# A transformer block on one core: the attention part recorded and then ordered by the builder for all five engines

## The chip, the core and the metric

The kernel runs on one core of one Trainium2 chip. The core has five instruction queues that run beside each other: TensorE (PE, matrix products and transpositions), VectorE (DVE), ScalarE (ACT), GpSimd (POOL) and SyncE (SP, which here only issues DMAs). Each engine runs its instructions in the order in which the program has them and waits at semaphores for results of the others. The metric is the device time of one execution in microseconds (us), the median of several runs.

## The reference

One block of an encoder: 512 tokens, 1024 features, float32, one layer. A normalisation and one input projection feed sixteen attention heads of three kinds; their outputs go through one output projection, then follow a gated MLP with a causal convolution and a gated per-layer embedding.

```python
hn = rms_norm(h, ln_mix[i])
z = hn @ w_in[i]
(q1, q2, k1, k2, va, qf, kf, vf, fg, qc, kc, vc) = jnp.split(z, IN_SPLITS, axis=-1)
...
o_a = diff_attention(q1, q2, k1, k2, va, lam, subln_gain[i], lam_init)
log_f = jax.nn.log_sigmoid(fg + fgate_bias[i])
o_b = forgetting_attention(qf, kf, vf, log_f)
o_c = chunk_attention(qc, kc, vc, rel_bias[i])
h = h + jnp.concatenate([o_a, o_b, o_c], axis=-1) @ w_out[i]
h = h + conv_gated_mlp(rms_norm(h, ln_ffn[i]), w_up[i], conv_w[i], conv_b[i], w_down[i])
gate = jax.nn.sigmoid(rms_norm(h, ln_ple[i]) @ w_ple_gate[i])
h = h + (p[i] @ w_ple_proj[i]) * gate
```

Every q and k is normalised per head. Group A (4 heads) takes the difference of two softmax maps, group B (6 heads) adds a cumulative sum of log forget gates to the scores, group C (6 heads) a bias by relative position.

## The kernel before

**Numbers.** Each float32 operand is split into a high and a low half of a faster type (`hi`, `lo`; `Th`, `Tl` for the tokens), and a product is three matmuls: hi hi, hi lo, lo hi (`mm3`). The high half of a weight is a cast on ScalarE; the low half is a subtraction on VectorE, on GpSimd, or a DMA that adds into the buffer (`load_w`, line 121 and on; the table entries "w..." say which).

**Stages.** First the input projection of the head pair A0, its weights in eight slices `WA`, while the tokens still arrive (`first_products`, line 289). The eight token blocks `xt` and the slices come by SP's queue (`load_k`, lines 245 to 250), slice 0 and the small columns by ACT's. All four token blocks' accumulators are open there, and slice k is used by twelve matmuls. Then nine more parts of the input projection (A0b, A1, A1b, B0 to B2, C0 to C2) in units of one part and one block of 128 tokens: eight steps of three matmuls each, then an evacuation with sums of squares (`qk_sums`, line 364: ACT squares, DVE sums, POOL scales and takes a power at line 373) and a scaling by DVE into `zn` (`qk_scale`). The steps of the heads are laid between the steps of these units: `qk_cols` turns q and k into columns by transpositions on PE (`split_q`, `split_k`, with moves on POOL at line 388), `scores` makes score products and softmax rows (the exponentials' tile is `e`; POOL scales it at lines 569 and 572), `prob_cols` transposes the rows (line 585), `values` multiplies them with V. `forget_cumsum` transposes the gates (`pf`), sums along the row on DVE (`fs`), sends the sums to DRAM and transposes them back (`pq`). The output projection `out_unit` runs in the same way in two column halves of four token blocks; its heads 12 to 15 come last (`last_out`). The MLP and the embedding behind it are recorded and ordered by a list scheduler of their own; the change doesn't touch them.

**What sets the order.** The table `T` gives for each step of a head its slot (a unit of a projection) and the place in it; `run` (line 691) deals them out. PE's order is the order in which the program is recorded, pinned instruction by instruction (`keep_in_program_order`). ACT and DVE are pinned only inside `first_products`; some DMAs are pinned too. For the rest the framework's scheduler chooses, with priorities: the table `EARLY` (line 726) and `step` raise those of some steps. Weights of the next part are loaded in pieces after each unit of this one. The buffers of the pools `ap` and `pi` and the accumulator banks are given out by the framework.

## Time and profile before

| what | value |
|---|---|
| median of 3 runs | 728.02 us (727.94 to 728.28) |
| profiled execution | 725.14 us |
| its span, first to last instruction | 723.4 us |
| granted clock of TensorE, mean | 0.999 |
| VectorE busy | 77% |
| ScalarE busy | 54% |
| GpSimd busy | 37% |
| DMA | 83.22 MB, mean 115 GB/s |

The profile is that of one execution. Its engine rows give the busy time of each engine; a row of the timeline gives the start, the length, the engine, the line and the tiles, and in brackets how long the engine was idle just before and what ended that. Nearly every instruction is recorded at one helper's line (78), so places are told by the tiles' names. From 4.4 to about 24 us runs the first projection, up to about 240 us the other projections with the heads, up to about 279 us the first part of the output projection with the last heads; behind it the rest of the output projection, the MLP and the embedding.

### The profile page before, as it was taken

What the parts mean: (1) busy time and instruction counts of PE and PEld (TensorE: products, weight loads), DVE (VectorE), ACT (ScalarE), POOL (GpSimd) and SP (SyncE); (2) the same over time, 40 slices, a digit from 0 to 9 for tenths busy, and PEclk for the clock granted to TensorE, in tenths of its full rate; (3) what the DMA queues carried; (4) which work ended last, traced back from release to release, by engine and by line L of the source; (5) the groups of instructions that cost most, each with busy time, mean ns of one, the idle gap of its engine ahead of it and who ended that gap; (6) DMA issues with size and microseconds to landing.
All of it is one profiled execution on the core that took longest, in us unless ns stands there. A gap on an engine that the chain in (4) does not pass through costs nothing. (4 is left out here: it accounts for less than half of the span.)

```text
span 723.4 us, 11848 instructions
## 1 busy us (share of the span) xinstructions
PE 703.0 (97%) x4204; PEld 631.1 (87%) x4204; DVE 555.8 (77%) x1090; ACT 393.9 (54%) x745; POOL 265.8 (37%) x355
## 2 busy tenths in 40 slices
PE   7998999999999999999999999999999999999997
PEld 7988889898999887889888899888998888899886
DVE  7788787987878845768969868787888779988552
ACT  6756676775666664565555444543444543544821
POOL 4675775756755540211102034021510004361400
PEclk9999999999999999999999999999999999999999
DMA  9544514414221145464445334552263322123541
GB/s 329 198 114 111 146 55 107 139 31 111 86 67 37 59 81 166 162 204 100 150 129 126 110 91 127 133 151 66 88 186 107 95 87 90 50 73 94 157 130 58
DMA packets 36950, 83.22 MB, mean 115 GB/s; under 512 B 4214, under 2 KB 6262, under 8 KB 36892
## 3 DMA queue, kind: packets, MB, share of 16 engines
q1 hardware_dynamic: 32844, 73.52, 32.3%
q0 software_dynamic: 3760, 8.66, 6.3%
q8 instruction: 33, 0.54, 0.3%
q10 hardware_dynamic: 288, 0.30, 0.1%
q14 instruction: 25, 0.20, 0.1%
HBM read 74.19 MB, written 4.21 MB: 108 GB/s over the span
## 5 line engine op out<-in xcount | busy, mean ns | idle before, releaser
L78 DVE TENSOR_TENSOR w_lo<-w_raw,w_hi 128x768 fp32r<-128x768 f32 (+1 forms) x118 | 113.9, 985 | 19.3 <-ACT w_hi L78 18.7
L78 ACT CAST w_hi<-w_raw 128x768 fp32r<-128x768 f32 (+1 forms) x118 | 89.6, 786 | 68.2 <-POOL w_raw L78 30.0
L78 PE MATMUL u<-Tl,w_hi 128*128 128x512 f32 (+1 forms) x336 | 125.5, 374 | 0.8 <-DVE Tl L78 0.8
L78 PE MATMUL u<-Th,w_hi 128*128 128x512 f32 (+1 forms) x336 | 125.7, 374 | 0.1
L78 PE MATMUL u<-Th,w_lo 128*128 128x512 f32 (+1 forms) x336 | 125.3, 373 | 0.0
L78 POOL TENSOR_TENSOR w_raw<-w_raw,w_raw 128x768 f32<-128x768 f32 (+1 forms) x30 | 53.9, 1818 | 148.4 <-DVE w_lo L78 116.1
L78 PEld LDWEIGHTS u<-Tl,w_hi 128*128 128x128 f32 x336 | 63.0, 188 | 13.0 <-DVE Tl L78 1.2
L78 PEld LDWEIGHTS u<-Th,w_lo 128*128 128x128 f32 x336 | 63.0, 188 | 12.6
L78 PEld LDWEIGHTS u<-Th,w_hi 128*128 128x128 f32 x336 | 63.0, 188 | 12.4 <-ACT pps L78 0.5
L78 DVE SCALAR_TENSOR_TENSOR c<-u,cols,c 128x511 f32<-128x511 f32 x76 | 56.7, 747 | 19.6 <-ACT c L78 18.4
L78 POOL DMA_DIRECT2D w_raw<-in_w_up_dram x9 | 7.9, 908 | 97.5 <-DMA w_raw<-in_w_up_dram 91.9
L78 ACT ACTIVATE c<-u,cols 128x512 f32<-128x512 f32 x38 | 29.5, 777 | 23.7 <-PE u L78 23.7
L78 PE MATMUL dn_X<-w_hi,g_ah 128*128 128x256 f32 x144 | 40.7, 283 | 0.3 <-DVE h L78 0.3
L78 PE MATMUL dn_X<-w_lo,g_ah 128*128 128x256 f32 x144 | 40.6, 282 | 0.3 <-DVE w_lo L78 0.3
L78 PE MATMUL dn_X<-w_hi,g_al 128*128 128x256 f32 x144 | 40.5, 281 | 0.0
L78 PE MATMUL B_z<-B_h,Th 128*128 128x384 f32 x96 | 34.5, 360 | 0.7 <-ACT B_l L78 0.7
L78 PE MATMUL C_z<-C_h,Th 128*128 128x384 f32 x96 | 34.3, 357 | 0.0
L78 PE MATMUL B_z<-B_h,Tl 128*128 128x384 f32 x96 | 32.3, 337 | 0.0
L78 PE MATMUL C_z<-C_h,Tl 128*128 128x384 f32 x96 | 32.3, 337 | 0.0
L78 PE MATMUL C_z<-C_l,Th 128*128 128x384 f32 x96 | 32.3, 336 | 0.0
L78 PE MATMUL B_z<-B_l,Th 128*128 128x384 f32 x96 | 32.3, 336 | 0.0
L78 PEld LDWEIGHTS dn_X<-w_hi,g_ah 128*128 128x128 f32 x144 | 27.1, 188 | 0.9 <-ACT w_hi L78 0.5
(482 smaller groups left out, 2139.1 us busy)
## 6 DMA issues: line engine op xcount, KB each, us to landing
w_raw<-in_w_up_dram SPq DMA_DIRECT2D x50, 384.0 KB, 3.8
w_raw<-in_w_down_dram SPq DMA_DIRECT2D x24, 384.0 KB, 3.1
w_raw<-in_w_up_dram SPq DMA_DIRECT2D x22, 256.0 KB, 3.5
B_r<-in_w_in_dram SPq DMA_DIRECT2D x12, 384.0 KB, 3.6
C_r<-in_w_in_dram SPq DMA_DIRECT2D x12, 384.0 KB, 3.2
wo_r<-in_w_out_dram SPq DMA_DIRECT2D x16, 256.0 KB, 2.9
w_raw<-in_w_ple_gate_dram SPq DMA_DIRECT2D x16, 256.0 KB, 3.0
h<-in_x_dram SPq DMA_DIRECT2D x4, 512.0 KB, 7.0
```

The costliest lines, as they stand in the source:

```text
L78: ins = getattr(self.eng, op)(*a, **k)
```

## The change

Every call on an engine between the first loads and the end of the attention part is now recorded in a plan instead of being issued (`Engine.__getattr__` and `Plan.add`). The plan keeps for each operation what it reads and writes by region, so what it depends on. `price` gives it a duration, on ACT and DVE 4% and on POOL 25% above its formula. `due` lays PE's operations end to end in recorded order and works back from there to the time by which each operation of another engine is due. `solve` then runs through time: the engine that is free first takes, of its ready operations, the one due first. PE takes only what has been ready for 0.15 us if there is such an operation, so it may pull later products ahead; ACT, DVE and POOL may hold back for a more urgent operation that is about to become ready. `emit` issues everything in that order and pins it, on all five engines. Three start values go with it: the times from which slice 0, the small columns and the identity are there, kept by the name of the tile.

The buffers come from `Fixed`: a fixed turn of tiles per tag, each held until its last reader. The table `EARLY`, the priorities and the waits for the first stage are gone. The loads of a part's weights are recorded after the units of the part before, not between them. The eight slices `WA` lie in other buffers: slices 0 and 1 in one `zn` tile, 2 and 3 in the other, the rest in tiles of the softmax rows. In `T` one entry moves, `A1v1` from (24, 7) to (24, 0).

Three places show how the order moves. The first is the head of SyncE's queue. `waq_92` is slice 1 before, `xbbias_86` the fifth block of tokens; after, `zn_91` holds slices 0 and 1, `zn_92` slices 2 and 3, and `bias_86` is the fifth block of tokens. Before:

```order
L249 DMA h<-in_xt_dram 128x257
L249 DMA h<-in_xt_dram 128x256
L249 DMA oall<-in_xt_dram 128x512
L250 DMA waq_92<-in_w_in_dram 128x384
L249 DMA oall<-in_xt_dram 128x512
L250 DMA waq_93<-in_w_in_dram 128x384
L249 DMA oall<-in_xt_dram 128x512
L250 DMA waq_94<-in_w_in_dram 128x384
L249 DMA xbbias_86<-in_xt_dram 128x512
```

and after:

```order
L261 DMA h<-in_xt_dram 128x257
L261 DMA h<-in_xt_dram 128x256
L261 DMA oall_71<-in_xt_dram 128x512 x2
L261 DMA zn_92<-in_w_in_dram 128x384
L261 DMA oall_71<-in_xt_dram 128x512
L261 DMA zn_92<-in_w_in_dram 128x384
L261 DMA bias_86<-in_xt_dram 128x512
L261 DMA zn_91<-in_w_in_dram 128x384
```

Slice 1 moves from the fourth load to the ninth. ScalarE casts it after the casts of slices 2 and 3 instead of ahead of them; PE's order of the first products is the same.

The second place is PE's queue at the forget sums (`pf`, `pq`; the banks of the changed kernel are named by their pool, `t_142` for the last of `pf`, `t_145<-ident,bias_87` for `pq`). Before:

```order
L78 MATMUL pf<-ident,oall 128x128 x4
L78 MATMUL A_z_787<-A_1_h,Th_64 128x384
L78 MATMUL A_z_787<-A_1_l,Th_64 128x384
L78 MATMUL A_z_787<-A_1_h,Tl_66 128x384
L78 MATMUL pq<-ident,fs 128x128 x4
```

and after:

```order
L261 MATMUL t_142<-ident,oall_71 128x128
L261 MATMUL z_125<-whi_102,Th_64 128x384
L261 MATMUL z_125<-wlo_103,Th_64 128x384
L261 MATMUL z_125<-whi_102,Tl_66 128x384
L261 MATMUL z_125<-whi_102,Th_64 128x384
L261 MATMUL z_125<-wlo_103,Th_64 128x384
L261 MATMUL z_125<-whi_102,Tl_66 128x384
L261 MATMUL z_125<-whi_104,Th_65 128x384
L261 MATMUL z_125<-wlo_105,Th_65 128x384
L261 MATMUL z_125<-whi_104,Tl_67 128x384
L261 MATMUL z_125<-whi_104,Th_65 128x384
L261 MATMUL t_145<-ident,bias_87 128x128 x4
```

Ten products of the projection stand between the two groups of transpositions where three stood. A little further on the probabilities of the first head are transposed. Before, block 3 of a bank follows block 2 at once:

```order
L78 MATMUL A_0_pt_865<-ident,A_0_0_e 128x128
L78 MATMUL A_0_pt_865<-ident,A_0_1_e 128x128
L78 MATMUL A_0_pt_865<-ident,A_0_2_e 128x128
L78 MATMUL A_0_pt_865<-ident,A_0_3_e 128x128
L78 MATMUL A1b_z_852<-A1b_h,Th_65 128x256
```

After, the blocks (`e_0_93`, `e_1_160`, `e_1_157`) alternate with products, score products follow, and block 3 (`e_0_95`) comes 20 rows after the first; the last rows of that stretch:

```order
L261 MATMUL z_124<-whi_112,Th_64 128x256
L261 MATMUL s_126<-kl_0_123,q_154 128x256
L261 MATMUL z_124<-wlo_113,Th_64 128x256
L261 MATMUL t_146<-ident,e_0_95 128x128
L261 MATMUL z_124<-whi_112,Tl_66 128x256
L261 MATMUL t_142<-ident,e_0_95 128x128
L261 MATMUL z_124<-whi_115,Th_65 128x256
```

The third place is PE's queue in the output projection, at the fifth of six steps of the first token block in the second column half (`wo_1_0` before, bank `z_124` after; `z_125` takes the next token block). Before:

```order
L78 MATMUL wo_1_0_3647<-wo_1_h,Th_64 128x512
L78 MATMUL wo_1_0_3647<-wo_1_l,Th_64 128x512
L78 MATMUL wo_1_0_3647<-wo_1_h,Tl_66 128x512
L78 MATMUL wo_1_0_3647<-wo_1_h,Th_65 128x512
L78 MATMUL wo_1_0_3647<-wo_1_l,Th_65 128x512
L78 MATMUL wo_1_0_3647<-wo_1_h,Tl_67 128x512
```

and after:

```order
L261 MATMUL z_124<-whi_104,Th_65 128x512
L261 MATMUL z_125<-whi_115,Th_64 128x512
L261 MATMUL z_125<-wlo_116,Th_64 128x512
L261 MATMUL z_125<-whi_115,Tl_66 128x512
L261 MATMUL z_125<-whi_118,Th_64 128x512
L261 MATMUL z_125<-wlo_119,Th_64 128x512
L261 MATMUL z_125<-whi_118,Tl_66 128x512
L261 MATMUL z_125<-whi_100,Th_64 128x512
L261 MATMUL z_125<-wlo_101,Th_64 128x512
L261 MATMUL z_124<-wlo_105,Th_65 128x512
L261 MATMUL z_124<-whi_104,Tl_67 128x512
```

Between the product with the high half `whi_104` and the one with its low half `wlo_105` now stand eight products of the next block.

```diff
--- before.py
+++ after.py
...
+class Plan:
+    WRITES = ("out", "accum_out")
+    LEAD = {"act": 0.035, "dve": 0.035, "pool": 0.095, "pe": 0.055, "sp": 0.1}
+    def __init__(self, clock, there):
+        self.group = "first"
+        self.clock, self.there, self.ops, self.mem = clock, {v.tensor.name: t for v, t in there}, [], {}
...
+    def add(self, eng, name, a, k):
+        op = Op(eng, name, a, k)
...
+        op.ready = 0.0
+        for w, v in sorted(seen, key=lambda x: x[0]):
+            r = self.region(v)
+            p0, p1, c0, c1 = r
+            log = self.mem.setdefault(v.tensor.name, [])
+            op.ready = max(op.ready, self.there.get(v.tensor.name, 0.0))
...
+        op.pos, op.group = len(self.ops), self.group
+        self.ops.append(op)
+        self.price(op)
+    def price(self, op):
+        e, k = op.eng.name, op.k
+        n = self.width(op.outs[0])
+        cols = sum(1 for v in op.ins if self.width(v) == 1) - (op.name == "reciprocal")
+        acc = "accum_out" in k
+        op.move = 0
+        if e == "pe":
+            if op.name == "transpose":
+                op.busy = 0.109
+            else:
+                op.busy = n * 0.0004556 + 0.001 if op.ins[0].dtype == F32R else n * 0.0017
+            op.lag = 0.165
+        elif e == "act":
+            op.busy, op.lag = 0.06 + n * 0.00088 + (0.18 + 0.04 * cols if acc else 0.09 * cols), 0.1
+        elif e == "dve":
+            n = max([n] + [self.width(v) for v in op.ins])
+            op.busy, op.lag = 0.07 + n * 0.001045 * (1 + (op.name == "tensor_tensor_scan")) + 0.06 * cols, 0.083
+        elif op.name == "dma_start":
+            op.move = n * 4 * op.outs[0].shape[0]
+            op.busy, op.lag = (0.9 if e == "pool" else 0.45), 0.0
+        elif op.name == "tensor_tensor":
+            op.busy, op.lag = ((0.42 + n * 0.155) if k["op"] == ALU.pow else (0.1 + n * 0.0024)), 0.04
...
+        else:
+            op.busy, op.lag = 0.08 + n * 0.00103 + (0.12 if n > 8 else 0.2) * cols, 0.04
+        op.busy *= self.SPARE.get(e, 1.0)
+    HW, SW, AT_ONCE = 0.385e6, 0.105e6, 8
+    SURE, AHEAD, MUCH, WAIT = 0.15, 1.0, 2.0, 0.6
+    SPARE = {"act": 1.04, "dve": 1.04, "pool": 1.25}
...
+    def due(self, shift):
+        t = 4.5
+        for op in self.ops:
+            if op.eng.name == "pe":
+                op.dl = t + shift.get(op.group, 0.0)
+                t += op.busy
+        for op in reversed(self.ops):
+            if op.eng.name != "pe":
+                spent = op.busy + op.lag + 0.05 + (op.move / self.HW + 2.0 if op.move else 0.0)
+                op.dl = min([q.dl for q in op.next], default=t) - spent
+    def solve(self):
+        clock = dict(self.clock)
+        free = {e: [] for e in self.ENGINES}
+        for op in self.ops:
+            op.left, op.at = len(op.deps), op.ready + self.LEAD[op.eng.name]
+            if not op.left:
+                free[op.eng.name].append(op)
+        wire, out, order = {"sp": 0.0, "pool": 0.0}, {"sp": [], "pool": []}, []
+        rank = lambda q: (q.dl, q.pos)
+        while True:
+            best = None
+            for e in self.ENGINES:
+                if free[e]:
+                    t = max(clock[e], min(q.at for q in free[e]))
+                    if best is None or t < best[0]:
+                        best = t, e
+            if best is None:
+                break
+            t, e = best
+            can = [q for q in free[e] if q.at <= t]
+            if e == "pe":
+                can = [q for q in can if q.at + self.SURE <= t] or can
+            op = min(can, key=rank)
+            if e not in ("pe", "sp"):
+                soon = [q for q in free[e] if t < q.at < t + op.busy * self.AHEAD and q.dl < op.dl - self.MUCH]
+                if soon:
+                    u = min(soon, key=rank)
+                    short = [q for q in can if t + q.busy <= u.at + 0.05]
+                    if short:
+                        op = min(short, key=rank)
+                    elif u.at - t < self.WAIT:
+                        op = u
+            free[e].remove(op)
+            t0 = max(clock[e], op.at)
+            busy = op.busy * (1.85 if e == "pe" and t0 < 8.6 else 1.0)
+            if op.move:
+                done = out[e]
+                if len(done) >= self.AT_ONCE:
+                    t0 = max(t0, done[-self.AT_ONCE])
+                wire[e] = max(t0 + 1.7, wire[e]) + op.move / (self.HW if e == "sp" else self.SW)
+                op.end = wire[e] + 0.6
+                done.append(op.end)
+            else:
+                op.end = t0 + busy + op.lag
+            op.start = t0
+            clock[e] = t0 + busy
+            order.append(op)
+            for q in op.next:
+                q.left -= 1
+                q.at = max(q.at, op.start if e == "pe" and q.eng is op.eng else op.end + self.LEAD[q.eng.name])
+                if not q.left:
+                    free[q.eng.name].append(q)
...
+        return order
+    def emit(self):
+        for op in self.ops:
+            for d in op.deps:
+                d.next.append(op)
+        for op in self.choose():
+            op.eng.now(op.name, op.a, op.k)
...
+    PLAN = []
     class Engine:
-        def __init__(self, eng):
-            self.eng, self.pinned, self.last = eng, False, None
+        def __init__(self, name, eng):
+            self.name, self.eng, self.pinned = name, eng, False
         def __getattr__(self, op):
             def do(*a, **k):
-                ins = getattr(self.eng, op)(*a, **k)
-                self.last = getattr(ins, "ins", None)
-                if self.pinned:
-                    tc.keep_in_program_order(ins)
-                return ins
+                if PLAN:
+                    return PLAN[-1].add(self, op, a, k)
+                return self.now(op, a, k, self.pinned)
             return do
...
+        def now(self, op, a, k, pinned=True):
+            ins = getattr(self.eng, op)(*a, **k)
+            if pinned:
+                tc.keep_in_program_order(ins)
+            return ins
+    pe, act, dve, pool, sp = (Engine(*e) for e in (("pe", nc.tensor), ("act", nc.scalar), ("dve", nc.vector), ("pool", nc.gpsimd), ("sp", nc.sync)))
+    class Fixed:
+        def __init__(self, pool, size={}, kind={}):
+            self.pool, self.size, self.kind, self.turn, self.made = pool, size, kind, {}, {}
+        def tile(self, shape, dt, tag, bufs=1, name=None):
+            i = self.turn[tag] = self.turn.get(tag, -1) + 1
+            key = tag, i % bufs
...
+            return v
...
+    banks = Fixed(ps)
     def bank(tag, name):
-        return ps.tile([P, 512], F32, tag=tag, bufs={"z": 2, "s": 2, "t": 3, "o": 1}[tag], name=name)
+        return banks.tile([P, 512], F32, tag, {"z": 2, "s": 2, "t": 3, "o": 1}[tag])
...
-    ap = p1.__enter__()
+    ap = Fixed(p1.__enter__())
...
-    WA = [ap.tile([P, S], F32, tag=tag, bufs=4, name=f"wa{tag}{i}")[:, :384] for tag in "qk" for i in range(4)]
-    def load_k(k, eng=nc.sync):
+    WA = [ap.tile([P, 1024], F32, tag="zn", bufs=2) for _ in range(2)]
+    WA = [t[:, i * 384 : (i + 1) * 384] for t in WA for i in range(2)]
+    WA += [ap.tile([P, n], F32, tag=tag, bufs=2)[:, :384] for tag, n in (("e2", 384), ("e2", 384), ("e3", 512), ("e3", 512))]
+    def load_k(k):
         parts = [(h[:, 3, c], xt0[:, c]) for c in (slice(0, H + 1), slice(H + 1, S + 1))] if k == 0 else [(XB[k], xt[k])]
         for dst, src in parts:
-            tc.keep_in_program_order(nc.sync.dma_start(out=dst, in_=src))
-        tc.keep_in_program_order(eng.dma_start(out=WA[k], in_=w_in[0][k // 2][:, k % 2, :]))
+            sp.dma_start(out=dst, in_=src)
+        if k:
+            sp.dma_start(out=WA[k], in_=w_in[0][k // 2][:, k % 2, :])
...
+    PLAN.append(Plan({"act": 2.95, "dve": 0.9, "pool": 1.0, "sp": 0.73, "pe": 1.0}, ((WA[0], 3.85), (cols, 4.6), (ident, 2.6))))
+    for k in range(KD):
         load_k(k)
...
-            qk_scale(z, ZN[pr, part], t, rs or evac())
+            rs = rs or evac()
+            if (pr, part) not in ZN:
+                ZN[pr, part] = ap.tile([P, NT, 2 * P], F32, tag="zn", bufs=2, name=f"{name}_zn")
+            qk_scale(z, ZN[pr, part], t, rs)
...
-        "A1v0": (22, 6), "A1s12": (21, 3), "A1p1": (23, 1), "A1v1": (24, 7), "A1n": (27, 7), "B0a": (22, 2),
+        "A1v0": (22, 6), "A1s12": (21, 3), "A1p1": (23, 1), "A1v1": (24, 0), "A1n": (27, 7), "B0a": (22, 2),
...
         for t in range(NT):
-            run(in_unit(pr, part, n, t, ws, pre[t]), steps.get(slot, []))
+            run(f"in{j}_{t}", in_unit(pr, part, n, t, ws), steps.get(slot, []))
             slot += 1
...
+        if j + 1 < len(PARTS):
+            q = PARTS[j + 1]
+            ws = [f() for f in in_w(j + 1, lo_by(q[0] + "ab"[q[1]], 4))]
+        else:
+            for k in range(6):
+                wo_load(k, 0)
...
+    PLAN.pop().emit()
```

More of the change, by code (lines that the diff above doesn't have):

```diff
@@ new lines, with again @@
+    class Fixed:
[4 more added lines that the diff above has]
+            key = tag, i % bufs
+            n = 1
+            for x in shape[1:]:
+                n *= x
+            if dt == BF16:
+                n //= 2
+            if key not in self.made:
+                kind = self.kind.get(tag, F32 if dt == BF16 else dt)
+                self.made[key] = kind, self.pool.tile([P, self.size.get(tag, n)], kind, tag=f"{tag}_{i % bufs}", name=f"{tag}_{i % bufs}")
+            kind, t = self.made[key]
+            v = t[: shape[0], :n]
+            if kind != dt:
+                v = v.bitcast(dt)
+            if len(shape) == 3:
+                v = v.rearrange("p (a b) -> p a b", a=shape[1])
+            return v
+        def again(self, tag, bufs, dt):
+            i = self.turn[tag] % bufs
+            return self.pool.tile([P, self.made[tag, i][1].shape[1]], dt, tag=f"{tag}_{i}", name=f"{tag}_{i}_again")
@@ L163, in in_turn @@
                 tag = ("hi", "lo")[(len(ring) - W["raw"]) % 2]
-            ring.append(pi.tile([P, 768], F32 if what == "raw" else F32R, tag=f"w{tag}", bufs=W[tag], name=f"w_{what}{len(ring)}"))
+            t = pi.tile([P, 768], F32 if tag == "raw" else F32R, tag=f"w{tag}", bufs=W[tag])
+            ring.append(t if tag == what else pi.again(f"w{tag}", W[tag], F32))
         else:
```

209 lines of the change are left out of this document (107 added, 102 removed), and 5 rows, old and new, of the table EARLY.

## The prediction

> **What bounds the kernel now.** I read the page's totals and slices first, then busy time by stretch, then what TensorE (PE) waits for.
>
> ```profile
> span 723.4 us, 11848 instructions
> PE 703.0 (97%) x4204; PEld 631.1 (87%) x4204; DVE 555.8 (77%) x1090; ACT 393.9 (54%) x745; POOL 265.8 (37%) x355
> PE   7998999999999999999999999999999999999997
> ```
>
> PE is busy 97% of the span, so a reordering that leaves every instruction in place can only win what PE waits, or lose by adding waits. The profiled execution took 725.14 us, 1.7 more than its span and 2.9 less than the median of 728.02; the sum below is made on 725.14 and the 2.9 are put back. The changed part ends on PE near 279 us; behind it the instruction sequence of PE is the same in both kernels.
>
> ```profile
> core 0: us, PE busy (x) PEld busy (x) DVE busy (x) ACT busy (x) POOL busy (x), PEclk, DMA share, GB/s
> 24.00:120.00 96.00, 90.95 (x591) 85.04 (x590) 80.09 (x227) 63.25 (x148) 63.75 (x90) 1.00 0.41 111
> 120.00:200.00 80.00, 78.20 (x482) 73.27 (x481) 66.55 (x219) 52.97 (x123) 55.67 (x83) 1.00 0.31 86
> 200.00:240.00 40.00, 39.88 (x247) 38.67 (x247) 32.20 (x95) 28.47 (x75) 22.55 (x40) 1.00 0.17 47
> 240.00:279.00 39.00, 37.65 (x196) 31.06 (x195) 22.53 (x54) 19.89 (x46) 15.72 (x22) 1.00 0.37 95
> 325.00:620.00 295.00, 294.67 (x1698) 257.03 (x1697) 242.94 (x334) 142.58 (x210) 58.83 (x41) 1.00 0.40 115
> ```
>
> From 24 to 279 us PE is seen idle for 5.05 + 1.80 + 0.12 + 1.35 = 8.3 us. That is not the whole, because a matmul's end is modelled and covers the beginning of a wait. What a matmul costs the queue is seen in a long run of them, and a transposition's cost in three that stand between products; two rows of scores show a covered wait.
>
> ```profile
> 543.23 50.41 PE u L78 x216
> 63.54 0.49 PE L78 MATMUL A_pt<-ident,A_e 128*128 128x128 f32 x3
> 63.78 0.37 PE L78 MATMUL A1b_z<-A1b_h,Th 128*128 128x256 f32 x1
> 63.99 0.28 PE L78 MATMUL A1b_z<-A1b_l,Th 128*128 128x256 f32 x1
> 202.87 0.34 PE L78 MATMUL C_s<-kl,C_q_q 128*128 128x384 f32 x1
> 203.32 0.50 PE L78 MATMUL C_s<-C_k_k,C_q_q 128*128 128x512 f32 x1
> 24.10 0.28 PE L78 MATMUL A0b_z<-A0b_h,Tl 128*128 128x262 f32 x1
> 278.92 0.39 PE L78 MATMUL wo<-wo_h,Tl 128*128 128x512 f32 x1
> ```
>
> 50.41 us for 216 matmuls of 512 columns is 0.2334 us each, 0.456 ns a column. From 63.54 to 63.99 stand three transpositions and one product of 256 columns (0.117): (0.45 - 0.117) / 3 = 0.11 us each. From 202.87 to 203.32 a product of 384 columns (0.175) took 0.45, so PE waited 0.27 us, of which the busy time shows 0.11. From the row at 24.10 to the one at 278.92 there are 1,259 products with 465,936 columns (744 of 384, 240 of 256, 187 of 512, 88 of 262) and 248 transpositions: 212.3 + 27.0 = 239.3 us of work in 255. **PE waits 15.6 us**: 9.4 from 24 to 120, 4.0 to 200, 0.3 to 240, 1.8 to 279. No one wait carries it:
>
> ```profile
> engine line waited for: us in total, times, longest us
> PE A_pt L78 <- DVE A_e L78: 1.3, 1, 1.3
> PE A1b_z L78 <- DVE A1b_zn L78: 1.0, 1, 1.0
> PE wo L78 <- DMA wo_l<-wo_r: 1.0, 1, 1.0
> PE B_s L78 <- DVE B_st L78: 0.9, 2, 0.6
> PE pq L78 <- DVE fs L78: 0.9, 1, 0.9
> ```
>
> **The change part by part.** No instruction is added or removed: the counts of all five engines are the same. The price lies in who waits, and in one load that comes later.
>
> *Waits of the attention part (15.6 us to win).* Three places that the order rows show. At the forget sums, PE in the old order has three products (0.52 us) between the transpositions `pf` and `pq`, and waits 0.9 us for the running sum; now ten stand there (10 x 0.175 = 1.75 us), more than 0.52 + 0.9. At the probabilities of the first head the fourth block was transposed right behind the other three, with a wait:
>
> ```profile
> 61.27 0.49 PE L78 MATMUL A_pt<-ident,A_e 128*128 128x128 f32 x3
> 63.01 0.33 PE L78 MATMUL A_pt<-ident,A_e 128*128 128x128 f32 x1 [1.25 <-DVE A_e L78]
> ```
>
> Now products of the next projection, scores, and the transpositions of the blocks at hand come first: about 15 products of 256 columns and six transpositions, 15 x 0.117 + 6 x 0.11 = 2.4 us, against a real gap of 63.01 - 61.27 - 0.33 = 1.4. At the output projection a low half came late by 1.0 us; now eight products of the next token block (8 x 0.233 = 1.9 us) are pulled ahead. These three are paid for, if the operands that PE is now given first are there; what could take their place is the next late one. So the unknown is the residue. Low end: 0.5 us, as in the stretch from 325 to 620, where VectorE is 82% busy (242.94 of 295) and PE idles only 0.33 us in 295. High end: all 15.6 come back elsewhere. In the first two stages VectorE is 83% busy, the same load, so the load does not force the waits; but there each head is a chain over four engines, and the engines follow an order fixed by estimated durations. I take one third of the 9.4 + 4.0, which is 4.5, and 0.5 for the last two stages: **5.0 us stay, 10.6 go**. This is a choice nearer to the row at 325.
>
> *The weights' second slice (a loss).* The first eight weight slices move to other buffers, two to a tile. The plan keeps "not there before 3.85 us" by tile, which was meant for the first slice; the second is in the same tile, and its load goes from fourth to ninth (counting the second half of xt0) in the queue of SyncE. PE's order at that point is unchanged: its thirteenth matmul needs that slice.
>
> ```profile
> 2.12 0.43 SPq L250 DMA_DIRECT2D waq<-in_w_in_dram  x1
> 4.45 1.65 PE L78 MATMUL A_z<-A_hi,Th 128*128 128x384 f32 x4 [4.45 <-ACT A_hi L78]
> 6.82 0.49 ACT L78 CAST A_hi<-waq 128x384 fp32r<-128x384 f32 x1
> 8.46 0.97 PE L78 MATMUL A_z<-A_hi,Th 128*128 128x384 f32 x4
> 9.14 0.51 ACT L78 CAST A_hi<-waq 128x384 fp32r<-128x384 f32 x1 [0.62 <-DMA waq<-in_w_in_dram]
> 10.16 0.72 ACT L78 ACTIVATE Th<-xbbias,cols 128x512 fp32r<-128x512 f32 x1 [0.50 <-DMA xbbias<-in_xt_dram]
> 10.65 0.86 PE L78 MATMUL A_z<-A_hi,Th 128*128 128x384 f32 x4
> ```
>
> In the old order the cast of this slice ran at 6.82, well ahead of PE's use at 8.46. The load that stood ninth (`xbbias`) landed at 10.16, by what waited for it. With the same loads ahead, the slice's cast begins at 10.16, ends at 10.65, and PE goes on near 10.7: 10.7 - 8.46 = **2.2 us lost**. PE has nothing else then, since all four accumulators wait for the same slice. The row at 9.14 is the wait for the load that stood eighth: no sooner than that, so at least 9.14 + 0.49 + 0.05 - 8.46 = 1.2 us.
>
> The first twelve matmuls took 8.46 - 4.45 = 4.0 us, 0.33 each; the next twelve, to 10.65, 0.18 each. If the pause makes PE slow again, twelve more cost 12 x 0.15 = 1.8 us, though the granted clock reads 1.00 in every stretch quoted, so the profile doesn't date the switch. The upper end of this term is 4.0. [...]
>
> *The rest.* Buffers held to their last reader, the loads of weights after a part instead of ahead of it, and scores moved by one slot add no work. What hides the loads is the queue's slack (DMA share 0.17 to 0.41 above). Without it one late load costs as much as `wo_l` did, 1.0 us; that lies within the residue. Behind 279 us the waits stay as they are.
>
> **Sum:** 725.14 - 15.6 + 5.0 + 2.2 = 716.7, with the 2.9 of the median: **719.6 us**.
>
> **Rivals.**
>
> *Nearly all waits go (0.10).* Residue 0.5 and only 1.2 at the head: 728.0 - 15.1 + 1.2 = 714.1. For it speaks the stretch at 325; against it the chains in the heads, with VectorE no less busy.
>
> *Late results of GpSimd come through (0.13).* The plan gives each operation of GpSimd one price; the chip doesn't:
>
> ```profile
> L572 POOL TENSOR_SCALAR B_e<-B_e,B_st 128x512 f32<-128x512 f32 x6 | 5.7, 957 | 1.6 <-DVE B_st L78 1.5
> 188.97 2.27 POOL L572 TENSOR_SCALAR B_e<-B_e,B_st 128x512 f32<-128x512 f32 x1 [0.79 <-DVE B_st L78]
> 182.54 0.69 POOL L572 TENSOR_SCALAR B_e<-B_e,B_st 128x512 f32<-128x512 f32 x1
> 126.92 1.59 POOL L373 TENSOR_TENSOR B_rs<-B_rs,nhalf 128x4 f32<-128x4 f32 x1
> L373 POOL TENSOR_TENSOR B_rs<-B_rs,nhalf 128x4 f32<-128x4 f32 x12 | 13.2, 1101 | 0.8
> ```
>
> The same scaling took 2.27 once and 0.69 otherwise, a power 1.59 against a mean of 1.10: about 2.1 us of lateness in the 80 us from 120 on, 6.7 in 255. If PE pays all of it beside the residue, the gain is 15.6 - 5.0 - 2.2 - 6.7 = 1.7; if it takes the residue's place, 6.7: 721.3 to 726.3, I say 725. Against it: the plan's price for the 512-wide scaling is 0.91 with its spare, over five of the six. [...]
>
> *The powers become the wait (slower, 0.20).* Every normalised q/k block passes one power on GpSimd, in the fixed order behind whatever the plan put ahead of it; 36 such blocks stand behind the first projection (the row of 12 above is B's). If each comes later than planned, PE's own order has no other work left at that point. It decides from (15.6 - 2.2) / 36 = 0.37 us a block; at 0.5, a scaling that stands ahead by mistake, PE loses 18.0 for the 15.6 it won: 728.0 - 15.6 + 2.2 + 18.0 = 732.6. Against it: the power's mean of 1.10 is under its planned 1.30, and GpSimd is 66% busy (63.75 of 96). That the order does not change at all is excluded by the rows of PE.
>
> **How the numbers follow.** The forecast has 0.57, with a range of its own from 715 to 725 (residue 0.5 to 10, head 1.2 to 4.0). The whole range, 713.0 to 729.5, leaves out most of the slower rival (0.16) and little below. What can't be told from no change is 0.2%, 1.5 us. Faster: 0.57 + 0.10 + 0.08 of the second rival = 0.75. The same: 0.03 of it and 0.02 of the third = 0.05. Slower: 0.02 + 0.18 = 0.20.
>
> **What would show it.** The thirteenth matmul near 10.7 us, waiting for a cast on ScalarE; it is wrong if it begins before 9.6. No wait over 0.3 us at the transpositions of the forget sums, at the fourth block of the first head, or at the output projection's low half. PE's visible idle from 24 us to the end of attention below 3 us instead of 8.3, and the end of that part near 271 instead of 279. Behind it the same stretches with the same idle time. It would be wrong if new waits for GpSimd's powers or scalings stood in the list of waits with over 5 us, or if PE's idle time behind the attention part grew.

## The result and the profile after

The changed kernel takes 722.52 us (median of 6 runs, 720.76 to 723.34), the kernel before 727.35 in the same comparison (6 runs, 726.08 to 728.28). The ratio is 0.9929, with a 95% interval of 0.9911 to 0.9947: 0.5 to 0.9% faster. The forecast was 719.6 with a range of 713.0 to 729.5. The profiled execution of the changed kernel, 723.34 us, is its slowest of six, that of the kernel before, 725.14, was faster than any of its six: between the two profiles only 1.8 us show.

The page of the changed kernel, its first lines:

```profile
span 721.6 us, 11821 instructions
...
PE 703.4 (97%) x4204; PEld 636.3 (88%) x4204; DVE 554.2 (77%) x1090; ACT 390.8 (54%) x745; POOL 277.3 (38%) x355
...
PE   6999999999999999999999999999999999989997
```

Against PE's row of before, three slices of 18 us differ: a 6 stands at the front for a 7 and an 8 in slice 36 for a 9, which are losses, and a 9 in slice 4 for an 8. The busy time by stretch shows where the gain is; columns as in the prediction:

```profile
core 0: us, PE busy (x) PEld busy (x) DVE busy (x) ACT busy (x) POOL busy (x), PEclk, DMA share, GB/s
4.45:24.00 19.55, 17.99 (x84) 17.48 (x85) 15.00 (x28) 14.86 (x28) 11.39 (x25) 1.00 1.04 385
24.00:120.00 96.00, 93.89 (x624) 90.91 (x623) 79.94 (x229) 62.45 (x151) 71.09 (x94) 1.00 0.42 110
120.00:200.00 80.00, 79.37 (x491) 75.20 (x490) 68.10 (x225) 52.72 (x130) 56.27 (x82) 1.00 0.30 86
200.00:240.00 40.00, 40.00 (x247) 38.68 (x246) 32.83 (x94) 28.41 (x73) 24.71 (x40) 1.00 0.21 60
240.00:279.00 39.00, 39.00 (x200) 32.67 (x198) 21.92 (x52) 20.09 (x45) 13.35 (x21) 1.00 0.39 97
...
620.00:680.00 60.00, 55.73 (x408) 53.04 (x407) 43.24 (x53) 30.46 (x48) 23.93 (x25) 0.94 0.24 76
```

From 24 to 279 us PE is seen idle for 2.11 + 0.63 = 2.7 us, where it was 8.3. With the covered part, worked out from the columns as in the prediction, PE waits 4.3 + 2.2 + 0 + 0, before rounding 6.4 us, where it waited 15.6. From 620 to 680 us it is busy for 55.73 us instead of 57.72, with a granted clock of 0.94: PE lost time in a stretch whose PE instructions are the same in both kernels.

How the two kernels stand at the same place in PE's queue (the difference is after minus before, so a minus sign means that the changed kernel is ahead):

| place in PE's queue | before, us | after, us | difference |
|---|---|---|---|
| 25th matmul | 10.65 | 13.70 | +3.05 |
| 101st matmul | 23.62 | 26.66 | +3.04 |
| 2594th from the end (end of the changed part) | 278.92 | 272.97 | -5.95 |
| 2200th from the end | 346.05 | 339.42 | -6.63 |
| 600th from the end | 625.34 | 618.71 | -6.63 |
| 540th from the end | 634.71 | 629.67 | -5.04 |
| 420th from the end | 649.85 | 648.12 | -1.73 |
| last matmul | 718.94 | 717.15 | -1.79 |

So three things happened: 3.0 us lost at the head, 9 us won in the attention part, and 4.9 of the 6.6 us given back between 618 and 648 us, long after it. Of the 4.9 us, 1.6 lie between the 600th and the 540th matmul from the end and belong to this one execution: the sixty matmuls took 10.97 us in it, in the kernel before and the eleven runs below 9.4 to 9.7. The other 3.3 us are a wait that the change brought, with the slow matmuls behind it. The loss at the head, in rows of the changed kernel's timeline (start and length in us; PE's first matmul, the load of slice 1, its cast, PE's thirteenth matmul, and the 23rd and 24th):

```profile
4.53 1.01 PE L261 MATMUL z<-whi,Th 128*128 128x384 f32 x2 [4.53 <-ACT whi L261]
...
4.81 0.43 SPq L261 DMA_DIRECT2D zn<-in_w_in_dram  x1
...
9.66 0.51 ACT L261 CAST whi<-zn 128x384 fp32r<-128x384 f32 x1 [0.72 <-DMA zn<-in_w_in_dram]
...
10.22 1.01 PE L261 MATMUL z<-whi,Th 128*128 128x384 f32 x2 [1.48 <-ACT whi L261]
...
13.35 0.51 PE L261 MATMUL s<-whi,Tl 128*128 128x384 f32 x2
```

The cast waits for the load as forecast and PE goes on at 10.22 instead of 8.46. From there to 13.35 stand ten matmuls in 3.1 us, 0.31 each on average, against 0.18 in the kernel before: nearly all of them run at 0.32, the rate of the first twelve. I call that the slow rate; the granted clock in the row from 4.45 to 24 us reads 1.00 and does not show it.

The loss in the tail, from the same timeline:

```profile
641.54 0.60 PE L261 MATMUL t<-ident,h 128*128 128x128 f32 x4
...
644.05 0.67 DVE L261 TENSOR_TENSOR h<-h,t 128x512 f32<-128x512 f32 x1
...
644.78 1.11 PE L261 MATMUL t<-ident,h 128*128 128x128 f32 x4 [2.64 <-DVE h L261]
...
645.91 0.41 PE L261 MATMUL z<-wlo,xh 128*128 128x256 f32 x1
...
647.61 0.41 PE L261 MATMUL z<-whi,xh 128*128 128x256 f32 x1
```

and the same place in PE's timeline of the kernel before:

```profile
646.58 1.04 PE L78 MATMUL n_t<-ident,h 128*128 128x128 f32 x8
...
647.57 0.28 PE L78 MATMUL dn_X<-w_lo,xh 128*128 128x256 f32 x1
...
649.85 0.55 PE L78 MATMUL n_t<-ident,h 128*128 128x128 f32 x3 [0.81 <-DVE h L78]
```

Before, eight transpositions for the last normalisation run at once, twelve products follow, and only the third group waits for `h`. After, the second group of four waits 2.6 us for VectorE to add the accumulator of the down projection to `h`. Its data are there, since before the change it ran at this place without a wait; its bank is not: the fixed turn of three banks gives it the one that the down projection has just filled (the runs with other banks below test this). The products behind the wait then take 0.21 us each (645.91 to 647.61: eight) instead of 0.12, a slow rate again; from 640 to 650 us the granted clock reads 0.83. The change of the buffers reaches past the attention part, since the accumulator banks of the MLP are taken from the same fixed turns.

### The profile page after: what moved, and what is told of

Same layout as the page of the kernel before. It is cut to its first block, busy times and chain, and to the rows that moved or that the text cites. A ratio compares the mean times of both kernels' runs of the same rounds, so it can differ in the third digit from the quotient of the medians.

```text
span 721.6 us, 11821 instructions
## 1 busy us (share of the span) xinstructions
PE 703.4 (97%) x4204; PEld 636.3 (88%) x4204; DVE 554.2 (77%) x1090; ACT 390.8 (54%) x745; POOL 277.3 (38%) x355
## 5 line engine op out<-in xcount | busy, mean ns | idle before, releaser
L261 PE MATMUL z<-whi,Th 128*128 128x384 f32 (+2 forms) x356 | 127.3, 364 | 7.4 <-ACT whi L261 6.0
L261 ACT CAST whi<-wraw 128x768 fp32r<-128x768 f32 (+2 forms) x132 | 98.4, 767 | 54.4 <-POOL wraw L261 23.4
L261 PE MATMUL z<-wlo,Th 128*128 128x384 f32 (+2 forms) x356 | 123.5, 353 | 0.3 <-DVE V L261 0.3
L261 PE MATMUL z<-whi,Tl 128*128 128x384 f32 (+2 forms) x356 | 122.3, 349 | 0.3 <-DVE V L261 0.3
L261 DVE TENSOR_TENSOR wlo<-wraw,whi 128x768 fp32r<-128x768 f32 (+2 forms) x114 | 105.9, 946 | 21.2 <-ACT whi L261 20.9
L261 PEld LDWEIGHTS z<-whi,Th 128*128 128x128 f32 x356 | 66.9, 190 | 12.1 <-ACT whi L261 6.5
L261 PEld LDWEIGHTS z<-wlo,Th 128*128 128x128 f32 x356 | 67.4, 190 | 4.4 <-DVE V L261 0.5
L261 PEld LDWEIGHTS z<-whi,Tl 128*128 128x128 f32 x356 | 67.0, 189 | 4.6 <-DVE V L261 0.6
L261 PE MATMUL z<-Th,whi 128*128 128x512 f32 (+1 forms) x180 | 66.2, 368 | 0.6 <-ACT pps L261 0.6
L261 PE MATMUL z<-Tl,whi 128*128 128x512 f32 (+1 forms) x180 | 66.1, 367 | 0.0
```

Source lines behind the costliest of these rows:

```text
L261: ins = getattr(self.eng, op)(*a, **k)
```

## The experiments

Each run is compared with the kernel before on the same chip, which took 726.3 to 726.7 there (727.35 in the comparison of the changed kernel). Between runs on different chips the ratios therefore say more than the medians; the ratios are those on record, not the quotients of the medians.

| kernel | median, us | ratio to before, 95% interval |
|---|---|---|
| changed kernel (its own comparison) | 722.52 | 0.9929 [0.9911, 0.9947] |
| slice 1 early | 720.57 | 0.9916 [0.9895, 0.9936] |
| a bank turn skipped | 720.04 | 0.9908 [0.9889, 0.9927] |
| both | 716.76 | 0.9868 [0.9851, 0.9885] |
| both, PE as recorded | 720.44 | 0.9918 [0.9904, 0.9931] |
| slice 1 early, banks exchanged | 716.91 | 0.9866 [0.9851, 0.9881] |
| the same, loads at 350 GB/s | 715.61 | 0.9846 [0.9831, 0.9861] |
| only PE and DMAs pinned | 738.23 | 1.0155 [1.0138, 1.0172] |
| no spare | 719.29 | 0.9898 [0.9882, 0.9915] |
| slice 1 late, banks exchanged, 350 GB/s | 719.91 | 0.9911 [0.9898, 0.9925] |
| three edits, no holding back | 717.71 | 0.9879 [0.9865, 0.9892] |
| three edits, 50% spare on GpSimd | 723.88 | 0.9964 [0.9950, 0.9977] |

**Slice 1 early.** The start time is held to the columns of slice 0:

```diff
-        self.clock, self.there, self.ops, self.mem = clock, {v.tensor.name: t for v, t in there}, [], {}
+        self.clock, self.there, self.ops, self.mem = clock, {v.tensor.name: (t, self.region(v)) for v, t in there}, [], {}
...
-            op.ready = max(op.ready, self.there.get(v.tensor.name, 0.0))
+            t, (q0, q1, d0, d1) = self.there.get(v.tensor.name, (0.0, r))
+            if p0 < q1 and q0 < p1 and c0 < d1 and d0 < c1:
+                op.ready = max(op.ready, t)
```

> The changed kernel with the start time 'not there before 3.85 us' held to the columns of slice 0 instead of to its whole tile, so that the load of slice 1 is fourth in SyncE's queue again; the rest of the order is nearly the same. Theory (the late slice costs what the head lost): PE's thirteenth matmul starts near 8.5 us instead of 10.2, the twelve that follow take 0.18 us each instead of 0.32, PE's 25th matmul starts near 10.7 instead of 13.7, and the kernel takes 3.0 us less than the changed one, about 719.5. Rival 1 (the queue of loads is full in any order, so the load that goes back to ninth is late instead): the thirteenth matmul at 8.5, but a wait of 1 us or more before the 49th, and less than 1 us gained in all. Rival 2 (the pause alone, the clock falls anyway): 1.8 us gained, with the slow matmuls still there.

The thirteenth matmul started at 8.32, the 25th at 10.41, at the fast rate of 0.17 us each: the head won its 3.3 us. But the 181st matmul started at 36.72, where the changed kernel had 36.27, and the attention part ended at 273.36 instead of 272.97. PE's waits from 24 to 279 us rose from 6.4 to 10.1 us: all that the head won was lost again by 37 us. About 1.6 of the 10.1 are slow matmuls behind the waits shown below (0.22 us for 262 columns instead of 0.12, granted clock 0.62 from 31.5 to 36 us), which this plan doesn't have in every execution. In the median the run is 2.0 us below the changed kernel, by the ratios 0.9, and the intervals overlap. This is rival 1 in its outcome, at another place than it said. First ScalarE's timeline of this run, then PE's:

```profile
22.67 0.19 ACT L263 ACTIVATION_READ_ACCUMULATOR e<-h 128x1 f32 x1
24.23 1.77 ACT L263 CAST whi<-wraw 128x768 fp32r<-128x768 f32 x2 [1.37 <-DMA wraw<-in_w_in_dram]
25.91 0.65 ACT L263 ACTIVATE e<-z 128x256 f32<-128x256 f32 x2
```

```profile
29.38 0.30 PE L263 MATMUL t<-ident,zn 128*128 128x128 f32 x1 [0.35 <-POOL rs L263]
...
30.17 0.33 PE L263 MATMUL t<-ident,zn 128*128 128x128 f32 x1 [0.36 <-DVE zn L263]
...
31.43 0.33 PE L263 MATMUL t<-ident,zn 128*128 128x128 f32 x1 [0.81 <-DVE zn L263]
```

The plan put two casts of the next part's weights ahead of the squares of the first projection. By its own prices it has those weights there at 21.5 and 22.6 us; ScalarE waits for the load until 24.23, and the squares, whose data were ready, stand behind it until 25.91. In the kernel before they ran at 23.25. So the powers and `zn` are late and PE waits. In the changed kernel the squares ran at 25.86, held by the late slice instead: the same time from another cause.

**A bank turn skipped, and both edits.** In the function that makes the transpositions of the last normalisation (`cols3`):

```diff
         def tr():
+            if (t, g) == (1, 0):
+                banks.turn["t"] += 1
```

> The changed kernel with one turn of the transposition banks skipped at the second transposition group of the last normalisation, nothing else. Theory (the fixed turn gives this group the bank that the down projection's first accumulator has just filled, and PE waits until VectorE has added it to h): in the changed kernel that group starts at 644.78 us of the profile, 2.8 us behind the first; now it starts right behind the first (0.45 us later), the twelve products behind it run ahead of the wait, and the kernel takes 3 us less than the changed one, about 719.5. Rival (the group waits for h itself, not for the bank): no difference over 0.5 us, the wait stays where it is.

> Both of these edits together. If both theories hold and the two places don't touch: 3.0 + 3.0 us less than the changed kernel, about 716.5. If the time that the head gains is lost again before the end, as the changed kernel lost 4.8 of the 6.6 us that it was ahead at 618 us: about 719.

In these two runs, and in the one with PE as recorded, the third group is written into the first group's bank before that is read, so the gate of one token block is computed from other columns, and a wait that belongs there is missing: they count as hints. The second group no longer waits; the stretch from 615 to 680 us holds 4.6 and 4.3 us of PE's waits where the changed kernel had 9.1. The bank alone took 720.04, 2.5 us below the changed kernel where 3 were expected, by the ratios 1.5, with intervals that overlap; its late slice came later still (thirteenth matmul at 11.16). Both together took 716.76, as the first case said.

**Banks exchanged.** The same without that flaw; the second and the third group swap banks:

```diff
         def tr():
+            k = {(1, 0): 1, (2, 0): -1}.get((t, g), 0)
+            banks.turn["t"] += k
             v["p"] = bank("t", f"n3_t{t}_{g}")
+            banks.turn["t"] -= k
```

> Slice 1 early, and the second and third transposition group of the last normalisation with their banks exchanged (instead of a turn skipped), so that no bank is taken before its last reader. Theory: the second group starts 0.45 us behind the first, the waits between 615 and 680 us are near 4.3 us as with the skipped turn, and the whole takes about 717, as the run with both edits did. Rival (the skipped turn was only fast because the first group's bank was overwritten too early): the wait comes back at the third group, and the kernel takes about 720.

716.91, and 4.3 us of waits in that stretch. PE's timeline reads as before the change:

```profile
639.14 1.03 PE L263 MATMUL t<-ident,h 128*128 128x128 f32 x8
...
640.13 0.27 PE L263 MATMUL z<-wlo,xh 128*128 128x256 f32 x1
...
642.41 0.66 PE L263 MATMUL t<-ident,h 128*128 128x128 f32 x4 [0.81 <-DVE h L263]
```

Against the run with slice 1 early alone this is 3.7 us less, and in that stretch of the profiles 3.3 us of waits are gone. The wait was for the bank.

**Loads at 350 GB/s in the plan.** ScalarE's timeline stands behind the expectation.

```diff
-    HW, SW, AT_ONCE = 0.385e6, 0.105e6, 8
+    HW, SW, AT_ONCE = 0.35e6, 0.105e6, 8
```

> The same, and the plan's rate for loads 350 instead of 385 GB/s. The order changes little; on ScalarE the squares of the first projection come ahead of two casts of the next weights that were planned ahead of them, because the plan has those weights there at 22.6 us where ScalarE waited for them until 24.2. Theory (a load later than planned holds ScalarE, so the squares, the powers and the normalised q and k are late, and this takes back what the head gained): the squares start near 23.3 us instead of 25.9, the first powers on GpSimd near 25 instead of 27.3, PE waits under 1 us instead of 2.0 at the three transpositions of zn after 28 us, PE's 181st matmul starts near 34 instead of 36.7, and the kernel takes 2.5 us less than with both edits, about 714. Rival (the powers on GpSimd bind there in any order): PE waits the same 2 us a little later, and under 0.7 us is gained.

```profile
22.80 0.64 ACT L263 ACTIVATE e<-z 128x256 f32<-128x256 f32 x2
...
23.66 0.77 ACT L263 ACTIVATE e<-s 128x256 f32<-128x256 f32 x2
24.32 0.82 ACT L263 CAST whi<-wraw 128x768 fp32r<-128x768 f32 x1
```

The squares ran at 22.80, ahead of the casts; the 181st matmul started at 33.28 and the attention part ended at 269.86, 2.4 us earlier than with both edits; 0.7 of these were there at the 101st matmul, ahead of the squares, since the slow rate at the start lasted longer in that execution (up to the fifteenth matmul, here up to the eleventh). The throughput does not explain why the load came late: from 4.45 to 24 us the run with slice 1 early moved 389 GB/s, more than the 385 of the plan. The 350 makes the plan expect loads later; why this one landed after its planned time stays open. The median is 1.3 us lower, half of what was expected, at 715.61: the fastest of these kernels, with all of the computation in it, 1.5% under the kernel before (0.9831 to 0.9861) and faster than the changed kernel.

**Slice 1 late again.** The kernel with loads at 350 GB/s and the banks exchanged, without the first edit.

> The changed kernel with the banks exchanged and the plan's rate for loads at 350 GB/s, but slice 1 late as in the changed kernel: the counterpart of the run with the slower loads, without its first edit. Theory (the late slice costs 3 us at the thirteenth matmul, and is felt at the end as soon as the casts no longer hold the squares; in the changed kernel the casts would have held them just as long): PE's 181st matmul starts near 36.3 us as in the changed kernel, against 33.3 with the slice early, and the kernel takes 2.5 to 3 us more than that run, about 718.3. Rival (the 3 us are made up by shorter waits later in the attention part): the end of that part within 1 us of that run, about 716.

719.91, 4.3 us more. The 181st matmul started at 38.40, 5.1 us later than at 33.28, and 5.0 us were still missing at the end of the attention part. The same late load that cost at most 2 us in the changed kernel costs 4.3 where the casts don't hold the squares (0.9 and 4.7 by the ratios). It was more than 3 because the load came 0.6 us later in this execution (thirteenth matmul at 10.84 instead of 10.22) and because the pause was followed by 18 slow matmuls, at 0.32 us each, instead of nine (PE's timeline, two matmuls a row):

```profile
8.02 0.84 PE L261 MATMUL s<-whi,Tl 128*128 128x384 f32 x2
...
10.84 1.01 PE L261 MATMUL z<-whi,Th 128*128 128x384 f32 x2 [1.98 <-ACT whi L261]
...
16.12 0.71 PE L261 MATMUL z<-wlo,Th 128*128 128x384 f32 x2
16.67 0.52 PE L261 MATMUL s<-wlo,Th 128*128 128x384 f32 x2
```

**Which engine's order wins.** PE is chained to the recorded order, in the first kernel; in the second nothing but PE and the DMAs is pinned.

```diff
     def emit(self):
+        line = [op for op in self.ops if op.eng.name == "pe"]
+        for a, b in zip(line, line[1:]):
+            if a not in b.deps:
+                b.deps.append(a)
```

```diff
-            op.eng.now(op.name, op.a, op.k)
+            op.eng.now(op.name, op.a, op.k, op.eng.name == "pe" or op.name == "dma_start")
```

> Both edits, and PE in the attention part kept strictly in the recorded order, as before the change; the other four engines are still ordered by the plan. Theory (the gain of the attention part, 9.2 us of PE's waits from 24 to 279 us, comes from PE taking later products while an operand is late): most of the waits come back, PE waits 13 us or more in that stretch, and the kernel takes 7 us more than with both edits alone. Rival (the gain comes from the order of VectorE, ScalarE and GpSimd, which now bring the operands in the order in which PE needs them): PE waits 8 us or less in that stretch and the kernel takes at most 2 us more.

> Both edits (banks exchanged); PE and the DMAs in the planned order, while the other operations of VectorE, ScalarE and GpSimd are handed over in the planned order but not pinned, so that the framework's scheduler may move them, without the priorities that it had before the change. Theory (what the change wins comes from the pinned order of the three other engines): PE waits 14 us or more from 24 to 279 us, and the kernel takes 4 us or more above both edits. Rival (PE's order carries it): PE waits 11 us or less there and the kernel takes within 1.5 us of both edits.

With PE as recorded: 720.44, 3.7 us above both edits (716.76), with 11.2 us of PE's waits from 24 to 279 us. With both edits the profile has 10.4 there, but that execution was its slowest by 2 us and had slow matmuls behind the waits at 30 us (mean granted clock 0.998, against 1.000 with the banks exchanged); with the banks exchanged, under the same plan, it is 8.3. Neither case was right; it lies between. With the other engines left to the framework's scheduler: 738.23, 21.3 us above 716.91. Its attention part ends at 292 us instead of 272. Its PE waits from 24 to 275 us grew to 26.1 us, from 8.3, and the list of them (us in total, times, longest) is led by VectorE:

```profile
PE s L263 <- DVE st L263: 5.3, 7, 1.1
PE z L263 <- DVE zn L263: 2.1, 2, 1.2
PE z L263 <- DVE V L263: 2.0, 2, 1.7
```

The kernel before had priorities in this place, which this run does not have, so the 21 us are not what the plan wins over the old order; they show that PE's look-ahead alone is worth nothing in this kernel when the other engines don't deliver in that order.

**The plan's numbers.** No spare, no holding back, more spare:

```diff
-    SPARE = {"act": 1.04, "dve": 1.04, "pool": 1.25}
+    SPARE = {}
```

> Both edits (banks exchanged), and the plan's durations without spare (VectorE and ScalarE without 4%, GpSimd without 25%). Theory (the spare on GpSimd keeps late scalings and powers from PE): PE waits 3 us or more above both edits from 24 to 279 us, the new waits being for GpSimd's results or for what stands behind them on VectorE, and the kernel takes 3 us more. Rival (the spare does not matter where GpSimd has idle time): within 1 us of both edits.

```diff
-    SURE, AHEAD, MUCH, WAIT = 0.15, 1.0, 2.0, 0.6
+    SURE, AHEAD, MUCH, WAIT = 0.15, 0.0, 2.0, 0.6
```

> All three edits (slice early, banks exchanged, loads at 350 GB/s), and the plan's holding back taken away: VectorE, ScalarE and GpSimd always take a ready operation and never wait for a more urgent one that is about to come. Theory (holding back keeps the chains of a head from standing behind a long cast or subtraction): PE waits 3 us or more above the run with the three edits, about 719. Rival (it decides little, the due times do the work): within 1 us.

```diff
-    SPARE = {"act": 1.04, "dve": 1.04, "pool": 1.25}
+    SPARE = {"act": 1.04, "dve": 1.04, "pool": 1.5}
```

> All three edits, and 50% spare on GpSimd instead of 25%. If the spare works because single results of GpSimd come up to 1.6 us late: another 1 us or more less, about 714.5. If 25% already covers what matters, and more only spoils the plan's times: the same or up to 3 us more.

No spare costs 2.4 us (719.29 against 716.91; PE's waits from 24 to 275 us 9.8 instead of 8.3), no holding back 2.1 (717.71 against 715.61; 8.4 instead of 6.6), and 50% spare on GpSimd costs 8.3 (723.88 against 715.61; 13.7 us of waits). The theories on no spare and on holding back were right in sign and somewhat too high in size; for more spare both cases were wrong, it loses far more than 3 us. Each of these edits moves rows on all engines, so their differences are those of whole orders; that a larger spare as such does harm is not shown by one value.

## Why the prediction came out as it did

The direction and the range were right, the size was not: 8.4 us were forecast and 4.8 measured (727.35 - 722.52). The range of 713.0 to 729.5 was wide enough to hold a loss that the prediction did not have in its sum. In the terms of the sum, from profile to profile: 725.14 - 15.6 + 6.4 (waits that stay) + 3.0 (head) - 0.7 (between 279 and 346 us) + 4.8 (tail) = 723.0, for 723.34 measured. This is the slowest of six executions, and 1.6 us of its tail are its own.

- *Waits of the attention part.* 5.0 of 15.6 us were to stay, 6.4 did. At the three places that were named the old waits are gone: none at the forget sums, none at the fourth block of the first head, none at the low half of the output projection. In the first two stages one third of 13.4 us, 4.5, was to stay, and nearly half did, 6.4; the last two stages kept nothing instead of 0.5. Visible idle time is 2.7 us, under the 3 that were named, and the attention part ends at 272.97 instead of near 271.
- *The head.* Mechanism right. PE waits for the cast from 8.4 to 10.22 us, 1.8 us later than before against 2.2 forecast; slow matmuls add 1.3, which the sum had left out, so the term is 3.0, inside its bounds of 1.2 to 4.0. That a pause of 2.2 us leaves the rate as it was, as the sum's 2.2 has it, no run shows: at this place nine slow matmuls followed 1.7 us, and eighteen followed 2.2 us with slice 1 late. What the sum did not see is that this loss was mostly not on the path: without it the casts of the next weights hold the same squares. As the kernel stands, slice 1 early is worth 2.0 us of the median or 0.9 by the ratios (intervals overlap). In its profile the attention part ended 0.4 us later than in the changed kernel, in the run with the banks exchanged, under the same plan, 0.7 earlier: it is not told apart from nothing.
- *"Behind 279 us the waits stay as they are."* This step failed, and it is the miss of the prediction; one of the signs that it had named for being wrong, a growth of PE's idle time behind the attention part, was seen. PE's sequence there is the same, but the bank of one transposition group is not. The change's edit of `bank` was taken as part of the attention part; the MLP calls the same function. It costs 3.3 us in the changed profile (from the 440th to the 420th matmul from the end 6.6 us instead of 3.3); the rest of the 4.8 is thirteen slow matmuls (0.21 us each instead of 0.12) after two waits between 620 and 623 us, 1.2, and a first wait there that was 0.3 longer. Only this execution has that rest, while the run with slice 1 early loses the time at the bank again (6.7 us for the same matmuls) and every run with another bank takes 3.3. What would have shown it ahead: the bank's name in the order rows of the tail, where the second group is `t_145<-ident,h`, the bank of the accumulator just above it.
- *The rivals.* That nearly all waits go did not happen. The powers did not become the wait. A late result of GpSimd stands in front of the longest wait left in the attention part, 1.4 us with its covered part (timeline of the changed kernel):

```profile
73.92 0.74 DVE L261 SCALAR_TENSOR_TENSOR e<-e,st,e 128x512 f32<-128x512 f32 x1
74.10 1.48 POOL L261 TENSOR_SCALAR rs<-rs,rstd 128x4 f32<-128x4 f32 x1 [0.46 <-DVE rs L261]
...
74.58 0.95 DVE L261 TENSOR_TENSOR wlo<-wraw,whi 128x768 fp32r<-128x768 f32 x1
...
76.72 0.48 DVE L261 SCALAR_TENSOR_TENSOR zn<-z,rstd,rs 128x256 f32<-128x256 f32 x1 [1.19 <-POOL rs L261]
...
77.35 0.36 PE L261 MATMUL z<-whi,Th 128*128 128x256 f32 x1 [1.27 <-DVE zn L261]
```

The mean of this operation over the attention part is 0.51 us (32 of them); half of them took at most 0.27. Here it took 1.48 and ended at 75.58, when VectorE's two operations shown beside it had run, the second until 75.53. Six runs with this order at this place (among them slice 1 early, banks exchanged and loads at 350 GB/s) show 1.48 again, so it belongs to the order and is no chance. What stretched it, no run shows. The rival's price of 6.7 us was more than four times this wait. Two longer rows of the same operation (1.62 us at 82.59, 1.69 at 105.89) ended in no wait of PE in the list of waits: those late results cost nothing.

## What to carry to other kernels

A loss that is certain where it stands is worth its price only after asking what would hold the same instruction next; here a late load and a queue of casts led to the same 25.9 us, and removing one showed next to nothing until the other was gone. When buffers get a fixed turn, every later user of the same pool changes its waits, so look at the places that the edit does not name. In an order fixed ahead on all engines, a load that lands later than planned holds everything behind its first reader (with slice 1 early two casts, whose weights the plan had at 21.5 and 22.6 us, began at 24.23, and the squares behind them at 25.91): take the time of a load from where its reader waited, not from the throughput of a busy stretch.

## What the runs showed of the hardware

The first matmuls of the kernel took 0.32 us for 384 columns, the later ones 0.17. Without a pause eleven were slow in the run with loads at 350 GB/s, thirteen in the kernel before, where the fast rate began 4.3 us after the first, and fifteen with the banks exchanged; the first and the last of these start with the same order. More slow matmuls stood behind pauses of PE. At the head, a pause of 1.7 us was followed by nine of them in the changed kernel and one of 2.2 us by eighteen with slice 1 late; with the bank turn skipped the fast rate had already begun, and a pause of 2.8 us was followed by twelve. In the tail, a pause of 2.8 us between two transposition groups was followed by slow ones in both profiles that have it (the changed kernel and slice 1 early): 0.21 instead of 0.12 us for 256 columns, for about 3 us.

In these profiles the length of a pause alone doesn't decide: one of 1.5 us stands at the same place of the tail in all thirteen, and only in the changed kernel did slow matmuls follow it (granted clock 0.66 from 624 to 629 us). The six runs of the changed kernel have mean granted clocks from 0.994 to 0.999 and spread over 2.6 us.
